# Final RMSNorm of a bidirectional encoder: products with the scale vector on VectorE between the small steps of 1/rms

## The chip, the cores and the metric

The kernel runs on one core of a Trainium2 chip. The metric is the device time of one execution in microseconds (us); lower is better. Engines are named as in the profile: PE is TensorE (matrix products), PEld its weight loads, DVE is VectorE, ACT is ScalarE, POOL is GpSimd, SP is SyncE, which here only starts transfers.

## The reference

Two encoder layers over 512 tokens of width 1024, in float32. Each layer adds three blocks to the residual stream x, and a norm ends it:

```python
for l in range(DEPTH):          # DEPTH = 2
    x = x + 0.5 * swiglu(rms_norm(x, ffn1_norm[l]), ffn1_w_in[l], ffn1_w_out[l])
    x = x + mixer(rms_norm(x, mix_norm[l]), ...)     # attention and a 2-D DFT, gated
    x = x + 0.5 * swiglu(rms_norm(x, ffn2_norm[l]), ffn2_w_in[l], ffn2_w_out[l])
return rms_norm(x, final_norm)

def rms_norm(x, g):
    y = x * rsqrt(mean(x * x, axis=-1) + 1e-6)
    return y * g
```

Only the end of it matters here: the last product of the last SwiGLU, which completes x, and the last `rms_norm`, whose result is the output. For each token that norm needs the sum of squares of all 1024 values before any of them can be scaled.

## The kernel before

**Layout.** x lies in SBUF as 128 partitions by 4 token blocks (`tb` 0 to 3) by 1024 columns; a column half `i` (0 or 1) has 512 columns. A token pair `j` is the blocks 2j and 2j+1. Every product is made from float32 values split into a high and a low part (`split`: ACT writes the high part at L288, DVE writes the difference at L289) and takes three matmuls (L282 high by high, L283 high activation by low weight, L284 low activation by high weight). A weight is loaded as a 128x1024 tile `raw` of 512 KB and split into `whi` and `wlo`, three buffers each, shortly ahead of its use (`Stream`, `Item.prep`).

**The last product.** The output product of the SwiGLU is made by Strassen's seven products, m = 1, 2, 5, 6, 7, 3, 4, each in three chunks c of the inner dimension (tiles c1h/c1l and so on are the split activations; `at` and `comb` at L593 make the sums that they are split from). `update` at L599 adds a finished product from PSUM to x, one token block at a time. Product 3 completes token blocks 2 and 3; product 4, the last, completes blocks 0 and 1 in column half 0, which is all that is then missing. Its third chunk runs `by_block`: the twelve matmuls of block 0 first, then the twelve of block 1.

**The final norm.** `nxt` is a `Norm` with `idx` 6. `squares` (L325, ACT, into `ssq`) sums squares of one block and one half. For blocks 2 and 3 `rstd` makes 1/rms (tile `r`) with an integer guess and three Newton steps on DVE, all on 128x2 tiles. For blocks 0 and 1 the generator `inverse` does the same on 128x1 tiles, in steps that other work can be put between. `gained` (L771) writes o = x * gf, where gf is the scale vector, fetched at L764; `scaled` (L776, ACT) multiplies o by 1/rms and starts the store of 256 KB from ACT's queue (L777); `whole` (L781, DVE) does both products in one instruction for the very last piece and stores from SP's queue (L782).

**Who sets the order.** Most instructions are put in order by a scheduler; inside `tc.manual_schedule` DVE and ACT keep the order in which the code is written, and `tc.high_priority` pulls a piece forward. In the kernel before, six `gained` products stand on POOL: four for blocks 2 and 3 and the second halves of blocks 0 and 1, written after chunk 0 of product 4; after them come the chain of `rstd` for blocks 2 and 3 and their four scalings. The manual block at the end holds blocks 0 and 1.

Of the kernel before, what the change touches and what calls it, by code (L numbers as in the profile page):

```python
# [9 lines left out]
F32 = mybir.dt.float32  # L10
# [3 lines left out]
AF = mybir.ActivationFunctionType  # L14
ALU = mybir.AluOpType
AX = mybir.AxisListType

P = 128
D = 1024
T = 512  # L20
# [7 lines left out]
EPS = 1e-6  # L28
# [64 lines left out]
def encoder_kernel(  # L93
    ctx: ExitStack, tc: tile.TileContext, xin, xtr, wst, gains, gfin, gbias, rpb, dft, chan, mask, ident_in, rot, out
):
    nc = tc.nc
# [16 lines left out]
    def slot(dt=F32, s="k", shape=(4, 256)):  # L113
        return kp.tile([P, *shape], dt, tag="k", name=nm(s), bufs=23)
# [39 lines left out]
    class Item:  # L154
# [9 lines left out]
        def prep(self):  # L164
            n = self.raw.n
            hi = wp.tile([P, 1024], F32R, tag="whi", name=nm("whi"), bufs=3)[:, 0:n]
            lo = wp.tile([P, 1024], F32R, tag="wlo", name=nm("wlo"), bufs=3)[:, 0:n]
            t = self.raw.t
            if self.add:
                V.tensor_tensor(t, t, self.add.t, ALU.add)  # L170
            if self.neg:
                S.activation(hi, t, AF.Copy, scale=-1.0)  # L172
                V.scalar_tensor_tensor(lo, t, -1.0, hi.bitcast(F32), ALU.mult, ALU.subtract)  # L173
            else:
                for c in range(0, n, n // self.parts):
                    cs = slice(c, c + n // self.parts)
                    split(hi[:, cs], lo[:, cs], t[:, cs])
            if self.then:
                G.dma_start(out=t, in_=wst[GRAN_AT[self.then]][:, 0:n], accum_op=ALU.add)
            self.out = (hi, lo)  # L180
# [65 lines left out]
    class Stream:  # L246
# [25 lines left out]
        def next(self):  # L272
            self.prep(self.pos + 1 + AHEAD)
            it = self.items[self.pos]
            self.pos += 1
            return it.out

    ws = Stream()
# [7 lines left out]
    def split(hi, lo, src, scale=None):  # L286
        if scale is None:
            S.activation(hi, src, AF.Copy)  # L288
            V.tensor_tensor(lo, src, hi.bitcast(F32), ALU.subtract)  # L289
        else:  # L290
            S.activation(hi, src, AF.Copy, scale=scale)
            V.scalar_tensor_tensor(lo, src, scale, hi.bitcast(F32), ALU.mult, ALU.subtract)


    def small(s, n=8):
        return sp.tile([P, 8], F32, tag=s, name=nm(s), bufs=2)[:, 0:n]

    def rsqrt(ms, n):
        r, t = small("r", n), small("rt", n)
        V.tensor_single_scalar(t.bitcast(I32), ms.bitcast(I32), 1, ALU.logical_shift_right)  # L300
        V.tensor_scalar(r.bitcast(I32), t.bitcast(I32), -1.0, float(0x5F3759DF), ALU.mult, ALU.add)
        for _ in range(3):
            V.tensor_tensor(t, r, r, ALU.mult)
            V.scalar_tensor_tensor(t, t, -0.5, ms, ALU.mult, ALU.mult)
            V.scalar_tensor_tensor(r, t, 1.5, r, ALU.add, ALU.mult)
        return r

    class Norm:

# [79 lines left out]
                V.tensor_scalar(r, t, 1.5, r, ALU.add, ALU.mult)  # L389
                yield  # L390

        def rstd(self, js=(0, 1)):

            n = 2 * len(js)
            a = 2 * js[0]
            ms = small("ms", n)
            with nullcontext() if self.idx == 6 else tc.high_priority():
                V.tensor_tensor(ms, self.ssq[:, a : a + n], self.ssq[:, 4 + a : 4 + a + n], ALU.add)
                V.tensor_scalar(ms, ms, 1.0 / D, EPS, ALU.mult, ALU.add)
                self.r = rsqrt(ms, n)  # L400
            if self.idx == 6:
                return self.r
            if self.mix:
                pc = bank()
                PE.matmul(pc[:, 0:2], mirror, self.r[:, 3:1:-1], start=True, stop=True)
                self.rflip = small("rflip", 2)
                V.tensor_copy(self.rflip, pc[:, 0:2])
                return
            self.rh, self.r2 = small("rh", 4), small("r2", 4)
            V.tensor_single_scalar(self.rh, self.r, 0.5, ALU.mult)  # L410
            V.tensor_tensor(self.r2, self.r, self.r, ALU.mult)
# [61 lines left out]
    def stage_ffn(norm, nxt, late):  # L473
# [122 lines left out]
        def update(ps, i, j, sign, bs=(0, 1)):  # L596
            for b in bs:
                v = x[:, 2 * j + b, i * T : (i + 1) * T]
                V.scalar_tensor_tensor(v, ps[b], 0.25 * sign, v, ALU.mult, ALU.add)  # L599
# [74 lines left out]
        for i, (m, c, _) in enumerate(steps):  # L674
            make(i)
            if i:
                make(i + 1)
            key = {6: 1, 4: 7}.get(m, m)
            if key not in ps:
                ps[key] = pair(f"o{key}")  # L680
            if m == 4 and c == 0 and nxt.mix:
                make(i + 2)
                ws.finish_stage()
                swap_pools(1)
            product(
                ps[key], made.pop(i), list(range(len(CHUNK[0][c]))), c == 0 and m in (1, 2, 3, 5, 7), c == 2,
                m in (4, 6), by_block=late and i == len(steps) - 1,
            )
            if i == 0:
                settle_at()  # L690
            if m == 4 and c == 0 and not late:
                with tc.manual_schedule(engines={mybir.EngineType.DVE, mybir.EngineType.Activation}):
                    make(i + 2)
                    nxt.quad(1, 1)
                    nxt.quad(0, 1)
            make(i + 2)
            if i == 6 and not late:
                nxt.quad(0, 0)
            if m == 4 and c == 1:
                update(ps[1], 1, 0, 1)  # L700
            if m == 4 and c == 0 and late:
                gains_of()
                for tb, i in ((2, 1), (3, 1), (2, 0), (3, 0), (0, 0), (1, 0)):
                    gained(G, tb, i)
                nxt.rstd((1,))
                for b in range(2):
                    nxt.inv[2 + b] = nxt.r[:, b : b + 1]
                    for i in (1, 0):
                        scaled(nxt, 2 + b, i)
            if c < 2:  # L710
                continue
            if m == 1:
                update(ps[1], 0, 0, -1)
            elif m == 2:
                update(ps[2], 0, 0, 1)
                nxt.squares(0, 0)
            elif m == 5:
                update(ps[5], 0, 1, 1)
                update(ps[5], 1, 1, -1)
            elif m == 6:  # L720
                update(ps[1], 1, 1, 1)
            elif m == 7:
                update(ps[7], 1, 1, 1)
                nxt.squares(1, 1)
                update(ps[1], 0, 1, -1)
            elif m == 3:
                update(ps[3], 0, 1, 1)
                nxt.squares(0, 1)
                if late:
                    make(i + 3)  # L730
            elif late:
                with tc.manual_schedule(engines={mybir.EngineType.DVE, mybir.EngineType.Activation}):
                    chain = [nxt.inverse(b) for b in range(2)]
                    for z in chain:
                        next(z)
                    update(ps[7], 1, 0, 1, (0,))
                    nxt.squares(1, 0, (0,))
                    gained(V, 0, 1)
                    next(chain[0])
                    update(ps[7], 1, 0, 1, (1,))  # L740
                    nxt.squares(1, 0, (1,))
                    for _ in chain[0]:
                        pass
                    scaled(nxt, 0, 0)
                    scaled(nxt, 0, 1)
                    for _ in chain[1]:
                        pass
                    scaled(nxt, 1, 0)
                    whole(nxt, 1, 1)
            else:  # L750
                update(ps[7], 1, 0, 1)
                nxt.squares(1, 0)
                nxt.later((1, 0))
# [1 line left out]
    gf = [None]  # L755
    ob = {}

    def half(tb, i):
        c = slice(i * T, (i + 1) * T)
        return ob[tb][:, c], x[:, tb, c], gf[0][:, c], out[:, tb, c]  # L760

    def gains_of():
        gf[0] = slot(F32, "gf", (D,))
        nc.sync.dma_start(out=gf[0], in_=bass.AP(tensor=gfin.tensor, offset=gfin.offset, ap=[[0, P], [1, D]]))  # L764

    def gained(engine, tb, i):

        if tb not in ob:
            ob[tb] = slot(F32, "o", (D,))
        o_, v, g, _ = half(tb, i)  # L770
        engine.tensor_tensor(o_, v, g, ALU.mult)  # L771

    def scaled(norm, tb, i):

        o_, _, _, to = half(tb, i)
        S.activation(o_, o_, AF.Copy, scale=norm.inv[tb])  # L776
        S.dma_start(out=to, in_=o_)  # L777

    def whole(norm, tb, i):
        o_, v, g, to = half(tb, i)  # L780
# [690 lines left out]
```

## Time and profile before

| | us |
|---|---|
| three timed runs | 1942.85, 1946.33, 1946.69 |
| median | 1946.33 |
| the profiled execution | 1946.85 |
| its span, first to last instruction | 1944.4 |
| outside the span | 2.45 |
| PE busy in the span | 1912.6 (98%) |
| DVE busy | 1624.1 (84%) |
| ACT busy | 1127.3 (58%) |
| POOL busy | 213.1 (11%) |

A busy PE row counts matmuls that overlap in the pipeline, so 98% is not the share of its peak. The times of rows below are us from the span's start. In a row of the timeline the first number is the start, the second the duration, then engine, line, operation, the tile written and those read, their shape, how many instructions were merged, and in brackets how long the engine had sat idle before it and what ended that. In a row of the waits view the numbers are the waited time in total, how often, and the longest. A row of the stretches view gives a stretch, its length, the busy time of each engine with its instructions, the granted clock of PE as a share of the full one, the share of time in which the 16 transfer engines moved data, and GB/s.

### The profile page before, as it was taken

The numbers are of one execution on the slowest core, as the hardware profiler recorded it, in microseconds if no ns is written. First come the engines' busy times: TensorE is split into PE (matmuls) and PEld (weight loads), VectorE is DVE, ScalarE is ACT, GpSimd is POOL, SyncE is SP. The second block draws the span as 40 slices with busy tenths as digits, with TensorE's granted clock in tenths as the row PEclk, the third lists the DMA queues.
The fourth block names the chain that finished last, engine by engine and source line by source line (L and its number), as shares of the span: only waits on it lengthen the run. The fifth ranks groups of instructions, "written<-read, shape, count | busy, mean of one in ns | idle before, by whom it ended". The sixth has DMA issues, their size and how long they took to land.

```text
span 1944.4 us, 24590 instructions
## 1 busy us (share of the span) xinstructions
PE 1912.6 (98%) x8997; PEld 1583.5 (81%) x8997; DVE 1624.1 (84%) x1945; ACT 1127.3 (58%) x1605; POOL 213.1 (11%) x252
## 2 busy tenths in 40 slices
PE   9999999999999999999999999999999999999996
PEld 7788888888778888888888888888887888888885
DVE  8878899698788877889977878996878887877998
ACT  6655666455556655566655556663555566555654
POOL 0001010300111010001000000102101110100012
PEclk9999999999999999999999999999999999999998
DMA  8777498321997567749857665965039975766692
GB/s 284 199 201 194 148 255 306 105 60 56 261 231 190 139 187 204 181 153 263 240 142 207 177 169 176 289 219 147 28 116 243 235 198 132 196 181 162 186 286 97
DMA packets 105448, 361.82 MB, mean 186 GB/s; under 512 B 12016, under 2 KB 14192, under 8 KB 105328
## 3 DMA queue, kind: packets, MB, share of 16 engines
q1 hardware_dynamic: 76848, 264.01, 39.7%
q0 software_dynamic: 27328, 94.39, 26.3%
q10 hardware_dynamic: 1152, 1.86, 0.3%
q8 instruction: 70, 1.15, 0.2%
q14 instruction: 50, 0.41, 0.1%
HBM read 354.97 MB, written 2.10 MB: 184 GB/s over the span
## 4 chain that ended last, share of the span: by engine, by line
PE 78%; DVE 13%; DMA 3%; issue 3%; ACT 3%; ACTq 0%; SPq 0%; POOL 0%; DVEq 0%; POOLq 0%
PE A L282 8%; PE A L284 8%; PE A L283 8%; PE o L283 5%; PE o L284 5%; PE o L282 5%; PE B L283 4%; PE B L284 4%; PE B L282 4%; PE ps L282 4%; PE ps L283 4%; PE ps L284 4%; DVE wlo L289 4%; DMA raw<-in_wst_dram 3%; PE C L283 2%
## 5 line engine op out<-in xcount | busy, mean ns | idle before, releaser
L289 DVE TENSOR_TENSOR wlo<-raw,whi 128x1024 fp32r<-128x1024 f32 (+1 forms) x522 | 628.1, 1209 | 252.9 <-ACT whi L288 251.9
L288 ACT ACTIVATE whi<-raw 128x1024 fp32r<-128x1024 f32 (+1 forms) x522 | 540.1, 1037 | 496.6 <-PE A L284 126.3
L152 POOL DMA_DIRECT2D raw<-in_wst_dram x152 | 131.2, 878 | 1338.4 <-DMA raw<-in_wst_dram 814.4
L170 DVE TENSOR_TENSOR raw<-raw,raw 128x1024 f32<-128x1024 f32 (+1 forms) x128 | 150.9, 1189 | 2.4
L283 PE MATMUL A<-wlo,xh 128*128 128x512 f32 x384 | 150.0, 391 | 2.8 <-DVE wlo L173 2.2
L284 PE MATMUL A<-whi,xl 128*128 128x512 f32 x384 | 149.6, 389 | 0.0
L282 PE MATMUL A<-whi,xh 128*128 128x512 f32 x384 | 149.4, 390 | 0.0
L172 ACT ACTIVATE whi<-raw 128x1024 fp32r<-128x1024 f32 x76 | 78.9, 1038 | 68.3 <-PE B L284 33.2
L173 DVE SCALAR_TENSOR_TENSOR wlo<-raw,whi 128x1024 fp32r<-128x1024 f32 x76 | 89.8, 1193 | 13.4 <-ACT whi L172 13.4
L283 PEld LDWEIGHTS A<-wlo,xh 128*128 128x128 f32 x384 | 72.1, 188 | 19.8 <-DVE wlo L173 4.0
L282 PEld LDWEIGHTS A<-whi,xh 128*128 128x128 f32 x384 | 71.9, 188 | 15.7 <-ACT whi L172 0.8
L284 PEld LDWEIGHTS A<-whi,xl 128*128 128x128 f32 x384 | 72.1, 188 | 14.9
L466 ACT ACTIVATE sn<-A 128x512 f32<-128x512 f32 x96 | 56.8, 598 | 41.8 <-PE A L284 41.7
L282 PE MATMUL A<-whi,t3h 128*128 128x512 f32 x192 | 75.1, 391 | 2.4 <-ACT sn L466 2.4
L282 PE MATMUL B<-whi,t1h 128*128 128x512 f32 x192 | 76.1, 398 | 0.4 <-ACT whi L288 0.4
L283 PE MATMUL A<-wlo,t2h 128*128 128x512 f32 x192 | 74.8, 390 | 0.5 <-DVE wlo L289 0.5
L283 PE MATMUL C<-wlo,xh 128*128 128x512 f32 x192 | 74.8, 390 | 0.5 <-DVE wlo L289 0.5
L283 PE MATMUL B<-wlo,t1h 128*128 128x512 f32 x192 | 75.0, 391 | 0.2
L282 PE MATMUL C<-whi,xh 128*128 128x512 f32 x192 | 74.8, 391 | 0.2 <-ACT whi L288 0.2
L282 PE MATMUL A<-whi,t2h 128*128 128x512 f32 x192 | 74.9, 392 | 0.0
L283 PE MATMUL A<-wlo,t3h 128*128 128x512 f32 x192 | 74.9, 390 | 0.0
L284 PE MATMUL B<-whi,t1l 128*128 128x512 f32 x192 | 74.9, 390 | 0.0
(352 smaller groups left out, 4944.1 us busy)
## 6 DMA issues: line engine op xcount, KB each, us to landing
raw<-in_wst_dram SPq DMA_DIRECT2D x463, 512.0 KB
raw<-in_wst_dram POOLq DMA_DIRECT2D x168, 512.0 KB, 7.8
raw<-in_wst_dram SPq DMA_DIRECT2D x30, 256.0 KB
vs<-v SPq DMA_DIRECT2D x12, 256.0 KB
bw<-in_rpb_dram SPq DMA_DIRECT2D x32, 68.0 KB
x<-in_xin_dram SPq DMA_DIRECT2D x4, 512.0 KB
raw<-in_wst_dram POOLq DMA_DIRECT2D x8, 256.0 KB, 8.4
dft<-in_dft_dram POOLq DMA_DIRECT2D x8, 256.0 KB, 5.4
```

The costliest lines, as they stand in the source:

```text
L152: G.dma_start(out=self.t, in_=wst[GRAN_AT[self.plus]][:, 0 : self.n], accum_op=ALU.add)
L170: V.tensor_tensor(t, t, self.add.t, ALU.add)
L172: S.activation(hi, t, AF.Copy, scale=-1.0)
L173: V.scalar_tensor_tensor(lo, t, -1.0, hi.bitcast(F32), ALU.mult, ALU.subtract)
L282: PE.matmul(ps, lh, rh, start=start, stop=False, skip_group_check=again)
L283: PE.matmul(ps, lh, rl, start=False, stop=False, skip_group_check=again)
L284: PE.matmul(ps, ll, rh, start=False, stop=stop, skip_group_check=again)
L288: S.activation(hi, src, AF.Copy)
L289: V.tensor_tensor(lo, src, hi.bitcast(F32), ALU.subtract)
L466: S.activation(t[:, b, :], ps[b], AF.Copy)
```

## The change

All six POOL products go to DVE. The chain of 1/rms for blocks 2 and 3 becomes a generator (`roots`, with a yield after every step of `rsqrt`), and the block at the end, which is now told to stand behind the split of the last weight (`issue_after` the last `wlo`), weaves the products between its steps: four products for blocks 2 and 3 in the first half of that chain, and those of block 0 and the first half of block 1 between the Newton steps of block 0. On ACT the squares of block 0 and of block 1 now stand ahead of the scalings; blocks 2, 3 and 0 are scaled by one 128x1024 instruction each instead of two of 128x512, and stored as 512 KB from SP's queue instead of twice 256 KB from ACT's. Block 1 keeps a half on ACT (`scaled`, stored from ACT's queue) and a half on DVE (`whole`, stored from SP's). The fetch of gf stays behind the last weight load in SP's queue. PE's instructions are the same and in the same order.

```diff
-    def rsqrt(ms, n):
-        r, t = small("r", n), small("rt", n)
+    def rsqrt(ms, r, t):
         V.tensor_single_scalar(t.bitcast(I32), ms.bitcast(I32), 1, ALU.logical_shift_right)
+        yield
         V.tensor_scalar(r.bitcast(I32), t.bitcast(I32), -1.0, float(0x5F3759DF), ALU.mult, ALU.add)
+        yield
...
             if m == 4 and c == 0 and late:
-                gains_of()
-                for tb, i in ((2, 1), (3, 1), (2, 0), (3, 0), (0, 0), (1, 0)):
-                    gained(G, tb, i)
-                nxt.rstd((1,))
-                for b in range(2):
-                    nxt.inv[2 + b] = nxt.r[:, b : b + 1]
-                    for i in (1, 0):
-                        scaled(nxt, 2 + b, i)
+                gf[0] = slot(F32, "gf", (D,))
+                nc.sync.dma_start(out=gf[0], in_=bass.AP(tensor=gfin.tensor, offset=gfin.offset, ap=[[0, P], [1, D]]))
...
-                with tc.manual_schedule(engines={mybir.EngineType.DVE, mybir.EngineType.Activation}):
+                with (
+                    tc.issue_after(ws.items[-1].last.ins),
+                    tc.manual_schedule(engines={mybir.EngineType.DVE, mybir.EngineType.Activation}),
+                ):
+                    ready = nxt.roots(2, 2)
+                    for tb, i in ((2, 0), (2, 1), (3, 0), (3, 1)):
+                        next(ready)
+                        gained(tb, i)
+                        next(ready)
                     chain = [nxt.inverse(b) for b in range(2)]
                     for z in chain:
                         next(z)
+                    for _ in ready:
+                        pass
+                    for b in range(2):
+                        nxt.inv[2 + b] = nxt.r[:, b : b + 1]
                     update(ps[7], 1, 0, 1, (0,))
                     nxt.squares(1, 0, (0,))
-                    gained(V, 0, 1)
+                    scaled(nxt, 2)
+                    gained(0, 0)
+                    next(chain[0])
+                    gained(0, 1)
+                    next(chain[0])
+                    gained(1, 0)
                     next(chain[0])
                     update(ps[7], 1, 0, 1, (1,))
                     nxt.squares(1, 0, (1,))
                     for _ in chain[0]:
                         pass
-                    scaled(nxt, 0, 0)
-                    scaled(nxt, 0, 1)
+                    scaled(nxt, 3)
+                    scaled(nxt, 0)
                     for _ in chain[1]:
                         pass
                     scaled(nxt, 1, 0)
...
-    def scaled(norm, tb, i):
+    def scaled(norm, tb, i=None):
         o_, _, _, to = half(tb, i)
         S.activation(o_, o_, AF.Copy, scale=norm.inv[tb])
-        S.dma_start(out=to, in_=o_)
+        (S if i is not None else nc.sync).dma_start(out=to, in_=o_)
```

More of the change, by code (lines that the diff above doesn't have):

```diff
@@ L176, in prep @@
                     cs = slice(c, c + n // self.parts)
-                    split(hi[:, cs], lo[:, cs], t[:, cs])
+                    self.last = split(hi[:, cs], lo[:, cs], t[:, cs])
             if self.then:
@@ L288, in split @@
             S.activation(hi, src, AF.Copy)
[L289 to L292, printed above, removed]
+            return V.tensor_tensor(lo, src, hi.bitcast(F32), ALU.subtract)
+        S.activation(hi, src, AF.Copy, scale=scale)
+        return V.scalar_tensor_tensor(lo, src, scale, hi.bitcast(F32), ALU.mult, ALU.subtract)
     def small(s, n=8):
         return sp.tile([P, 8], F32, tag=s, name=nm(s), bufs=2)[:, 0:n]
-    def rsqrt(ms, n):
-        r, t = small("r", n), small("rt", n)
+    def rsqrt(ms, r, t):
         V.tensor_single_scalar(t.bitcast(I32), ms.bitcast(I32), 1, ALU.logical_shift_right)
+        yield
         V.tensor_scalar(r.bitcast(I32), t.bitcast(I32), -1.0, float(0x5F3759DF), ALU.mult, ALU.add)
+        yield
         for _ in range(3):
             V.tensor_tensor(t, r, r, ALU.mult)
+            yield
             V.scalar_tensor_tensor(t, t, -0.5, ms, ALU.mult, ALU.mult)
+            yield
             V.scalar_tensor_tensor(r, t, 1.5, r, ALU.add, ALU.mult)
-        return r
+            yield
     class Norm:
@@ L390, in inverse, with roots, rstd @@
                 yield
[L392 to L402, printed above, removed]
+        def roots(self, a, n):
+            ms, self.r, t = small("ms", n), small("r", n), small("rt", n)
+            V.tensor_tensor(ms, self.ssq[:, a : a + n], self.ssq[:, 4 + a : 4 + a + n], ALU.add)
+            yield
+            V.tensor_scalar(ms, ms, 1.0 / D, EPS, ALU.mult, ALU.add)
+            yield
+            yield from rsqrt(ms, self.r, t)
+        def rstd(self):
+            with tc.high_priority():
+                for _ in self.roots(0, 4):
+                    pass
             if self.mix:
@@ L735, in stage_ffn @@
                         next(z)
+                    for _ in ready:
+                        pass
+                    for b in range(2):
+                        nxt.inv[2 + b] = nxt.r[:, b : b + 1]
                     update(ps[7], 1, 0, 1, (0,))
                     nxt.squares(1, 0, (0,))
-                    gained(V, 0, 1)
+                    scaled(nxt, 2)
[4 more added lines that the diff above has]
+                    gained(1, 0)
                     next(chain[0])
@@ L756, in encoder_kernel, with half, gained @@
     ob = {}
-    def half(tb, i):
-        c = slice(i * T, (i + 1) * T)
+    def half(tb, i=None):
+        c = slice(0, D) if i is None else slice(i * T, (i + 1) * T)
         return ob[tb][:, c], x[:, tb, c], gf[0][:, c], out[:, tb, c]
[L762 to L766, printed above, removed]
+    def gained(tb, i):
         if tb not in ob:
@@ L770, in gained @@
         o_, v, g, _ = half(tb, i)
-        engine.tensor_tensor(o_, v, g, ALU.mult)
-    def scaled(norm, tb, i):
+        V.tensor_tensor(o_, v, g, ALU.mult)
+    def scaled(norm, tb, i=None):
         o_, _, _, to = half(tb, i)
         S.activation(o_, o_, AF.Copy, scale=norm.inv[tb])
-        S.dma_start(out=to, in_=o_)
+        (S if i is not None else nc.sync).dma_start(out=to, in_=o_)
     def whole(norm, tb, i):
```

## The prediction

> **What bounds the kernel now.** I read the page first: PE is busy for 98% of the span, and the chain that ended last is 78% PE. Only the last 40 us differ between the two kernels, so I turned to the waits of that stretch. PE waits there once, and it is the longest wait of PE in the whole span:
>
> ```profile
> PE o L283 <- DVE wlo L289: 5.3, 1, 5.3
> ACT whi L288 <- DVE ms L399: 6.1, 1, 6.1
> ACT o L776 <- DVE r L305: 4.3, 1, 4.3
> ```
>
> Next, DVE's timeline there, and POOL's:
>
> ```profile
> 1908.63 3.22 DVE L289 TENSOR_TENSOR wlo<-raw,whi 128x1024 fp32r<-128x1024 f32 x2
> 1911.77 1.22 DVE L593 TENSOR_TENSOR at<-at,at 128x1024 f32<-128x1024 f32 x1
> 1912.90 1.28 DVE L599 SCALAR_TENSOR_TENSOR x<-o,x 128x512 f32<-128x512 f32 x2
> 1914.10 1.94 DVE L593 TENSOR_TENSOR at<-at,at 128x1024 f32<-128x1024 f32 x1
> 1915.96 2.28 DVE L289 TENSOR_TENSOR c4l<-at,c4h 128x1024 fp32r<-128x1024 f32 x1
> 1918.16 2.28 DVE L289 TENSOR_TENSOR wlo<-raw,whi 128x1024 fp32r<-128x1024 f32 x1
> 1920.37 2.29 DVE L289 TENSOR_TENSOR c4l<-at,c4h 128x1024 fp32r<-128x1024 f32 x1
> 1922.58 1.21 DVE L289 TENSOR_TENSOR wlo<-raw,whi 128x1024 fp32r<-128x1024 f32 x1
> ```
>
> ```profile
> 1907.76 3.54 POOL L771 TENSOR_TENSOR o<-x,gf 128x512 f32<-128x512 f32 x2 [19.54 <-DMA gf<-in_gfin_dram]
> 1913.66 7.92 POOL L771 TENSOR_TENSOR o<-x,gf 128x512 f32<-128x512 f32 x4 [2.37 <-DVE x L599]
> ```
>
> The reader is to see one pair: a two-input DVE instruction of 128x1024 takes 1.22 us in POOL's pause (1911.30 to 1913.66) and 2.28 us while a POOL product runs. DVE is delayed by POOL, PE waits for the `wlo` that ends at 1920.44, and while it waits its clock is halved:
>
> ```profile
> 1915.25:1917.90 2.65, 0.00 (x0) 0.00 (x0) 2.65 (x2) 1.88 (x3) 2.65 (x2) 1.00 0.00 0
> 1917.90:1920.50 2.60, 0.00 (x0) 0.00 (x1) 2.60 (x3) 1.12 (x2) 2.60 (x2) 0.50 0.00 0
> 1920.50:1924.70 4.20, 4.20 (x10) 3.33 (x11) 4.20 (x4) 0.00 (x0) 1.08 (x1) 0.50 0.00 0
> ```
>
> Last, ACT's end, which sets the last stores:
>
> ```profile
> 1933.99 0.63 ACT L325 ACTIVATE junk<-x 128x512 bf16<-128x512 f32 x1 [0.41 <-ACT o L776]
> 1936.53 0.63 ACT L325 ACTIVATE junk<-x 128x512 bf16<-128x512 f32 x1 [1.81 <-DVE x L599]
> 1940.66 0.34 ACTq L777 DMA_DIRECT2D out_dram<-o  x1
> ```
>
> The update of block 0 starts at 1930.51, but its squares only at 1933.99, behind four scalings with their store starts.
>
> **Part 1, POOL's products go.** From 1908.63 I lay DVE's unchanged order out again, at 1.13 us from start to start for 128x1024 and 0.60 for 128x512 (durations 1.22 and 0.68 less the overlap of 0.08). The split pair at 1908.63 takes 1.73, `at` starts at 1910.36, the two updates of x at 1911.49, the second `at` at 1912.69, c4l at 1913.82, `wlo` at 1914.95; it ends at 1916.16 where it ended at 1920.44. ACT keeps up: its `whi` for this one starts at 1910.80, held by PE, in both. PE's wait of 5.25 us becomes 0.97 (1915.25 to 1916.22). PE waited 0.99, 0.91 and 0.90 us at 53, 1466 and 506 us, and the granted clock there is 1.00, so I expect no halved clock. Ten matmuls then need 2.3 us (0.227 from start to start) and not 4.3, and the last `whi`, which waits for their buffer, starts at 1918.75, was 1925.10.
>
> DVE goes on: c4l 1916.08, two `wlo` to 1919.47, an update of x, the last `wlo` 1920.07 to 1921.20, an update, free at 1921.80. The last `whi` is ready at 1919.83, 0.24 before DVE asks for it. PE ends block 0's matmuls at 1924.1 (was 1930.48).
>
> **Part 2, what DVE takes on.** In the changed order 21 instructions stand between 1921.80 and the update of block 0: four products and 17 small steps. A product costs 0.60 (row 1931.24: 0.69 long). A small step that needs the one before it costs 0.20 (L303 to L305 at 1929.25, 1929.44, 1929.64), another 0.07 (1928.67, 1928.73). Nine dependent, seven others and the last 0.07: 2.40 + 1.80 + 0.56 = 4.76. The bounds are 17 at 0.07 and 17 at 0.20, so 3.6 to 5.8. The update starts at 1926.56, 2.5 us after PE is ready: DVE, not PE, is late next. Against 1930.51 the gain here is 3.95.
>
> One rule speaks against taking work back. The Trainium skill, "Perfetto Trace Analysis", section "Optimizing Scalar/DVE Operations", says that a saturated DVE may be relieved to ScalarE or even GpSimd, but warns that the two share a read port. Here the pair 1.22 and 2.28 sides with the warning.
>
> **Part 3, ACT and the chains.** Block 0: squares start 0.72 after the update (1935.81 to 1936.53), `ms` 0.75 later (1933.99 to 1934.74), at 1928.03. Its chain with two products between the Newton steps: 1.07 + 0.60 + 0.43 + 0.60 + 0.43 = 3.13, so block 1's update starts at 1931.16 (was 1935.81), PE long done. Product (0,0) hides behind the squares. Squares of block 1: 1931.88 to 1932.61, `ms` 1932.63 (was 1937.40).
>
> Queued behind those squares on ACT, though ready since 1926.5, is the scaling of block 3. No row shows 128x1024 with a scale per partition; 0.72 for half plus 0.42 (1.04 less 0.62, the splits L288) gives 1.14, between 1.04 and 1.44. Block 3 is scaled to 1933.76, block 0 to 1934.9. Added wait: block 1's tile `r` takes over the buffer that holds blocks 2 and 3's 1/rms, so its first write (ready 1933.07) waits for block 3's scaling, to 1933.80; the rest of its chain is queued behind. From there 1.86 (1937.83 to 1939.69): `whole` and ACT's half start at 1935.66, their stores at 1936.46.
>
> **Part 4, the stores.** Before, 1 MB is left for the end, now 1.57 MB: 512 KB of block 3 started at 1933.82, 512 KB of block 0 at 1934.95, two halves of block 1 at 1936.46. SP has nothing else queued; its three starts cost ACT nothing, where ACT lost 0.42 per store. Data follows 0.85 after the start. This stretch gives the rate:
>
> ```profile
> 1941.35:1942.75 1.40, 0.00 (x0) 0.00 (x0) 0.00 (x0) 0.00 (x0) 0.00 (x0) 0.50 0.96 363
> ```
>
> At full share that is 378 GB/s. Data from 1934.67, never out of work: 1.57 MB takes 4.16, to 1938.83, which also covers the added wait by 0.13. From the last data (1942.84) to the end were 1.56: the span ends at 1940.39. Bounds for the stores: no limit by rate, 1939.56; 290 GB/s, as the stretch 1932 to 1934 moved with its pauses, 1941.65.
>
> **Sum.** 1944.40 to 1940.39 is a gain of 4.0 us: 3.95 up to block 0's update, 0.8 more to block 1's `ms`, 0.7 given back by the stores. From the profiled execution's own 1946.85 that is 1942.85. It stands 0.5 above the median, so 1942.3 against 1946.33.
>
> A measurement of this kernel can tell about 0.2%, 3.9 us, from no change. My gain sits on that line.
>
> **Rivals.**
>
> *A, the gain is there but under the line (chance 0.27).* Stores at 290 GB/s: gain 2.75. All small steps at 0.20: gain 3.0. Both and 1.44 per scaling: 1.4, so 1944.9. For it: three sizes that no row shows. Against: each is taken from the nearest row.
>
> *B, the halved clock isn't in every run of before (0.18).* The three runs differ by 3.8 us, which speaks for something that comes and goes. Without the drop the last `whi` is 2 us earlier, but then DVE's `ms` at 1924.92 is ahead of the last `wlo`: that starts at 1924.99 for 1926.19, 1.2 us gained. If the median run had no drop, the gain is 2.8: 1943.5. The Trainium skill, "TensorE: Matmul & The Clock Gate", section "What's actually happening", says the clock falls after one idle window of about 3.4 us that runs freely. By that an idle time of 5.25 us holds a whole window only in some runs, and 0.97 in none; this trace agrees with one drop, 2.65 us into the wait, and none at 0.99. Should the drop stay in the changed kernel, its last `wlo` comes 1.8 later: 1944.1.
>
> *C, slower: the 2.28 isn't POOL's doing (0.06).* If DVE's two-input instructions are slow at that place for another reason, part 1 gives nothing: DVE is free at 1927.93 as before, and the six products on its path cost 2.24 each. Then block 0's update starts at 1927.93 + 4.76 + 4 x 1.62 = 1939.2, and with two more slow products the end lies 11.8 later: 1958. It decides from 0.92 us per product. Against it: the 1.22 in POOL's pause, and DVE's own product at 1931.24 with 0.69.
>
> That the change doesn't take place is excluded by the order of the instructions: POOL has no product left, PE's order is the same.
>
> **Numbers.** Forecast, a gain from 3.9 up: 0.47, with the bounds 3.6 for part 2 and 1939.56 for the stores up to 5.9 us, 1940.4. A and B: 0.45 together, C and what I overlook: 0.08. Faster 0.47, within 0.45, slower 0.08. Range: 1940.4 less 1.2 for runs like the fast one shown, 1939.2, to A's 1944.9 plus 0.9, 1945.8; C stays out.
>
> **What would show it.** DVE rows of 1.21 from 1908 to 1922; PE's wait near 1 us at clock 1.00; DVE's update of block 0 near 1926.6, behind 21 instructions without a wait; block 3's scaling right behind block 1's squares; SP's stores near 1933.8 and 1935, data without a pause. It is wrong if the two-input rows stay above 2, if PE's clock drops, or if a store starts after 1937.

## The result, and the profile after

| | before | changed |
|---|---|---|
| median of 22 runs each, us | 1944.55 | 1941.66 |
| lowest to highest | 1942.49 to 1950.29 | 1939.12 to 1945.16 |
| the profiled execution | 1946.85 | 1942.89 |
| its span | 1944.4 | 1940.9 |

The ratio of the times is 0.9981, 95% interval 0.9975 to 0.9987. At 1944.55 that is 3.7 us gained, between 2.5 and 4.9; the two medians differ by 2.9. So the change is a gain beyond doubt, but on which side of 0.2% it lies these runs do not tell.

The two profiled executions do not reach the end at the same pace: a row that the change does not touch, DVE's three merged updates of x ahead of the last weights, starts at 1906.83 before and at 1907.58 changed. I take that row as **the mark** and count from it: 37.57 us to the end of the span before, 33.27 changed, so 4.3 us gained behind the mark (the expectations below write 33.32, reckoned from the span as rounded in the table). A time of the prediction is to be compared with a row of the changed kernel less 0.75.

DVE's timeline of the changed kernel (line numbers have moved: the updates of x are L605, the products L784, the last piece L794):

```profile
1907.58 1.88 DVE L605 SCALAR_TENSOR_TENSOR x<-o,x 128x512 f32<-128x512 f32 x3
1909.38 1.82 DVE L289 TENSOR_TENSOR wlo<-raw,whi 128x1024 fp32r<-128x1024 f32 x2
1913.45 1.22 DVE L599 TENSOR_TENSOR at<-at,at 128x1024 f32<-128x1024 f32 x1
1914.58 1.22 DVE L289 TENSOR_TENSOR c4l<-at,c4h 128x1024 fp32r<-128x1024 f32 x1
1915.72 1.22 DVE L289 TENSOR_TENSOR wlo<-raw,whi 128x1024 fp32r<-128x1024 f32 x1
...
1922.59 0.15 DVE L398 TENSOR_TENSOR ms<-ssq 128x2 f32<-128x2 f32 x1
...
1927.31 0.68 DVE L605 SCALAR_TENSOR_TENSOR x<-o,x 128x512 f32<-128x512 f32 x1
...
1931.97 0.68 DVE L605 SCALAR_TENSOR_TENSOR x<-o,x 128x512 f32<-128x512 f32 x1
1933.50 0.21 DVE L386 TENSOR_SCALAR ms<-ssq,e 128x1 f32<-128x1 f32 x1 [0.85 <-ACT junk L328]
...
1934.54 0.15 DVE L389 TENSOR_SCALAR r<-rt 128x1 int32<-128x1 int32 x1 [0.51 <-ACT o L789]
...
1936.40 0.75 DVE L794 SCALAR_TENSOR_TENSOR o<-x,r,gf 128x512 f32<-128x512 f32 x1
```

Every 128x1024 row is back at 1.22. From 1922.59 to 1927.31 stand the 21 instructions that DVE took on; the two updates behind them belong to blocks 0 and 1. The two bracketed rows are the only idle times shown here: one for the squares, one for the buffer of `r`. Two rows of the waits view of this stretch:

```profile
PE o L283 <- DVE wlo L289: 1.0, 1, 1.0
...
DVE r L389 <- ACT o L789: 0.5, 1, 0.5
```

PE's wait of 5.3 us has become 1.0. The stretches view (length, busy time of PE, PEld, DVE, ACT and POOL, then PE's clock, the share of time with data, GB/s):

```profile
1915.00:1920.00 5.00, 4.01 (x18) 3.02 (x17) 5.00 (x5) 3.02 (x4) 0.00 (x0) 1.00 0.00 0
1920.00:1925.00 5.00, 5.00 (x24) 4.14 (x23) 4.93 (x12) 0.70 (x1) 0.00 (x0) 1.00 0.00 0
```

```profile
1935.37:1939.54 4.17, 0.00 (x0) 0.00 (x0) 1.65 (x5) 0.90 (x2) 0.00 (x0) 0.50 0.96 377
```

The clock stays at 1.00 through the stretch where it was halved, POOL is at 0, and the last stores run without a pause at 377 GB/s. ACT's timeline of the end shows squares in front and scalings behind:

```profile
1928.09 0.63 ACT L328 ACTIVATE junk<-x 128x512 bf16<-128x512 f32 x1 [7.39 <-DVE x L605]
1928.72 1.13 ACT L789 ACTIVATE o<-o,r 128x1024 f32<-128x1024 f32 x1
1932.75 0.63 ACT L328 ACTIVATE junk<-x 128x512 bf16<-128x512 f32 x1 [2.90 <-DVE x L605]
1933.38 2.17 ACT L789 ACTIVATE o<-o,r 128x1024 f32<-128x1024 f32 x2
```

Block 0's squares start 0.78 us after its update starts; it was 3.48 (1930.51 to 1933.99).

### The profile page after: what moved, and what is told of

Its sections match the earlier page's. It is cut to its first block, busy times and chain, and to the rows that moved or that the text cites. A ratio compares the mean times of both kernels' runs of the same rounds, so it can differ in the third digit from the quotient of the medians.

```text
span 1940.9 us, 24584 instructions
## 1 busy us (share of the span) xinstructions
PE 1911.7 (98%) x8997; PEld 1582.2 (82%) x8997; DVE 1621.7 (84%) x1951; ACT 1126.2 (58%) x1602; POOL 201.8 (10%) x246
## 4 chain that ended last, share of the span: by engine, by line
PE 77%; DVE 14%; issue 3%; DMA 3%; ACT 2%; POOL 0%; ACTq 0%; DVEq 0%; POOLq 0%
PE A L282 8%; PE A L284 8%; PE A L283 8%; PE B L283 4%; PE B L284 4%; PE o L283 4%; PE B L282 4%; PE o L284 4%; PE o L282 4%; DVE wlo L289 4%; PE ps L282 4%; PE ps L283 4%; PE ps L284 4%; DMA raw<-in_wst_dram 3%; PE C L283 2%
## 5 line engine op out<-in xcount | busy, mean ns | idle before, releaser
L283 PE MATMUL B<-wlo,xh 128*128 128x512 f32 x192 | 74.8, 390 | 0.1
```

The lines of the kernel that those rows point to most:

```text
L283: PE.matmul(ps, lh, rl, start=False, stop=False, skip_group_check=again)
```

## The experiments

All of them are counted from the same mark, each in one profiled execution. The last two columns are the ratio to the kernel before in timed runs on the same chip, and the number of runs.

| kernel | update of block 0 | block 1's squares | end of span | ratio (95%) | runs |
|---|---|---|---|---|---|
| before | 23.68 | 29.70 | 37.57 | 1 | 22 |
| before, second profile | 23.48 | 29.50 | 37.37 | | 1 |
| before, third profile | 23.83 | 29.21 | 37.07 | | 1 |
| changed | 19.73 | 25.17 | 33.27 | 0.9981 (0.9975 to 0.9987) | 22 |
| changed, second profile | 19.72 | 25.16 | 33.28 | 0.9982 (0.9973 to 0.9990) | 11 |
| products on DVE, ACT as before | 19.72 | 28.99 | 36.86 | 1.0003 (0.9994 to 1.0011) | 11 |
| ACT changed, products on POOL | 24.01 | 28.99 | 37.11 | 0.9992 (0.9982 to 1.0001) | 11 |
| block 3 scaled early | 19.73 | 25.17 | 32.74 | 0.9980 (0.9971 to 0.9989) | 11 |
| updates first | 17.46 | 21.11 | 31.60 | 0.9972 (0.9961 to 0.9984) | 6 |
| updates first, again | 17.45 | 21.09 | 31.59 | 0.9973 (0.9962 to 0.9984) | 7 |

My theory: POOL's products slow DVE, DVE holds PE, and beside that ACT's scalings hold block 0's squares; the change removes both. Rivals: the gain belongs to one of the two alone; or POOL is not what slows DVE (C); or it comes from the clock only and so comes and goes (B).

**Products on DVE, ACT as before.** Half of the change is undone: blocks 2 and 3 are again scaled in four halves, with ACT starting their stores, ahead of block 0's squares, and block 0 in two halves. The order on ACT, the whole-block scalings and the stores from SP's queue thus go together; no run here tries them apart.

```diff
                         nxt.inv[2 + b] = nxt.r[:, b : b + 1]
+                    for b in range(2):
+                        for i in (1, 0):
+                            scaled(nxt, 2 + b, i)
                     update(ps[7], 1, 0, 1, (0,))
                     nxt.squares(1, 0, (0,))
-                    scaled(nxt, 2)
...
-                    scaled(nxt, 3)
-                    scaled(nxt, 0)
+                    scaled(nxt, 0, 0)
+                    scaled(nxt, 0, 1)
```

> DVE's order and products as in the changed kernel, POOL without products; but ACT again scales blocks 2 and 3 in four halves ahead of block 0's squares and stores all halves but one from its own queue, as before. Measure: from the start of DVE's three merged updates of x ahead of the last splits (1906.83 before, 1907.58 changed) to the end of the span: 37.57 us before, 33.32 changed. My theory: DVE rows stay at 1.22, PE's wait at 1 us, the update of block 0 at 19.7 from the mark as in the changed kernel; then four scalings with a store start each (1.14 apiece, row 1937.57 to 1938.71) hold block 0's squares 3.9 us longer, so 36.6: nearly all of the gain goes. Rival, that taking POOL's products away is the gain and ACT's order a detail: 33.3 to 34.5. Rival C, two-input DVE instructions are slow at that place whatever POOL does: rows of 2.28.

Measured: 36.86 from the mark to the end, so 0.71 gained of 4.3; in timed runs no difference that the interval can tell. DVE's timeline and, behind it, ACT's:

```profile
1915.10 1.22 DVE L289 TENSOR_TENSOR wlo<-raw,whi 128x1024 fp32r<-128x1024 f32 x1
...
1926.69 0.68 DVE L605 SCALAR_TENSOR_TENSOR x<-o,x 128x512 f32<-128x512 f32 x1
...
1932.12 0.21 DVE L386 TENSOR_SCALAR ms<-ssq,e 128x1 f32<-128x1 f32 x1 [4.14 <-ACT junk L328]
```

```profile
1930.98 0.34 ACTq L792 DMA_DIRECT2D out_dram<-o  x1
1931.36 0.63 ACT L328 ACTIVATE junk<-x 128x512 bf16<-128x512 f32 x1 [0.41 <-ACT o L791]
```

The update of block 0 comes as early as in the changed kernel (19.72), and then DVE waits 4.14 us for squares that stand behind four scalings. In one point the kernel is not as before. There ACT's scalings ran in pairs with the store starts behind them:

```profile
1930.48 1.34 ACT L776 ACTIVATE o<-o,r 128x512 f32<-128x512 f32 x2 [4.33 <-DVE r L305]
1932.24 1.34 ACT L776 ACTIVATE o<-o,r 128x512 f32<-128x512 f32 x2 [0.42 <-ACT o L776]
```

Four took 3.51 us (1930.48 to 1933.99); here a store start stands behind each, and they take 4.55 (1926.81 to 1931.36). So 1.04 us of its loss is due to the order that I wrote, and not to the change.

**ACT changed, products on POOL.** The other half undone: six products on POOL again, ACT and SP as in the changed kernel. The Newton steps on DVE keep the order of the changed kernel too.

```diff
                 nc.sync.dma_start(out=gf[0], in_=...)
+                for tb, h in ((2, 1), (3, 1), (2, 0), (3, 0), (0, 0), (1, 0)):
+                    gained(tb, h, G)
...
                     ready = nxt.roots(2, 2)
-                    for tb, i in ((2, 0), (2, 1), (3, 0), (3, 1)):
-                        next(ready)
-                        gained(tb, i)
-                        next(ready)
...
-                    gained(0, 0)
...
-                    gained(1, 0)
...
-    def gained(tb, i):
+    def gained(tb, i, engine=V):
...
-        V.tensor_tensor(o_, v, g, ALU.mult)
+        engine.tensor_tensor(o_, v, g, ALU.mult)
```

> The six products back on POOL where they stood, ACT's order, the whole-block scalings and SP's stores as in the changed kernel. Same measure (37.57 before, 33.32 changed). My theory: DVE rows of 2.28 again, PE's wait 5.25 with the halved clock if the free-running window falls so, the update of block 0 24.0 from the mark as before; then block 0's squares at once, but the stores of 1.57 MB start at 30.6 and take 4.2, so 37.2: hardly any gain. Rival, that ACT's order and the stores are the gain: 34 to 35. The clock row also shows whether the drop is in every execution.

Measured: 37.11, which is 0.46 less than in the first profile of the kernel before and no less than in its third (37.07); so no gain is shown, and the timed runs show none that the interval can tell. DVE's timeline, POOL's, the waits and the stretches of this kernel:

```profile
1906.19 1.87 DVE L605 SCALAR_TENSOR_TENSOR x<-o,x 128x512 f32<-128x512 f32 x3
1907.98 2.90 DVE L289 TENSOR_TENSOR wlo<-raw,whi 128x1024 fp32r<-128x1024 f32 x2
1910.81 1.21 DVE L599 TENSOR_TENSOR at<-at,at 128x1024 f32<-128x1024 f32 x1
...
1915.00 2.29 DVE L289 TENSOR_TENSOR c4l<-at,c4h 128x1024 fp32r<-128x1024 f32 x1
1917.21 2.28 DVE L289 TENSOR_TENSOR wlo<-raw,whi 128x1024 fp32r<-128x1024 f32 x1
```

```profile
1906.66 2.55 POOL L780 TENSOR_TENSOR o<-x,gf 128x512 f32<-128x512 f32 x2 [18.91 <-DMA gf<-in_gfin_dram]
1912.70 7.92 POOL L780 TENSOR_TENSOR o<-x,gf 128x512 f32<-128x512 f32 x4 [3.50 <-DVE x L605]
```

```profile
PE o L283 <- DVE wlo L289: 4.6, 1, 4.6
```

```profile
1917.00:1919.50 2.50, 0.00 (x0) 0.00 (x0) 2.50 (x3) 1.06 (x2) 2.50 (x2) 0.77 0.00 0
1919.50:1923.70 4.20, 4.15 (x10) 3.28 (x11) 4.20 (x3) 0.00 (x0) 1.13 (x1) 0.50 0.00 0
```

With the products back on POOL, the rows of 2.28, PE's wait and the halved clock are back, in another kernel and on another run. Rival C is out from both sides: these rows take 1.22 in every kernel without POOL's products, and 2.28 beside them in every kernel with them. The squares of block 0 now follow its update at once, but that update comes at 24.01.

**The two halves and the whole.** The path up to block 1's squares, cut into its stretches (each is the difference of two starts). Three starts of the kernel before, the two updates and the last product:

```profile
1930.51 0.69 DVE L599 SCALAR_TENSOR_TENSOR x<-o,x 128x512 f32<-128x512 f32 x1
1935.81 0.68 DVE L599 SCALAR_TENSOR_TENSOR x<-o,x 128x512 f32<-128x512 f32 x1
1939.69 0.75 DVE L781 SCALAR_TENSOR_TENSOR o<-x,r,gf 128x512 f32<-128x512 f32 x1
```

| us | before | changed | products on DVE only | ACT only |
|---|---|---|---|---|
| mark to update of block 0 | 23.68 | 19.73 | 19.72 | 24.01 |
| on to its squares (ACT) | 3.48 | 0.78 | 4.67 | 0.79 |
| on to `ms` | 0.75 | 0.75 | 0.76 | 0.75 |
| on to update of block 1 (DVE) | 1.07 | 3.13 | 3.13 | 2.66 |
| on to its squares | 0.72 | 0.78 | 0.71 | 0.78 |
| sum | 29.70 | 25.17 | 28.99 | 28.99 |

The change gains twice, 3.95 on DVE and PE and 2.70 on ACT, and pays 2.06 in the fourth row: two products and two more Newton steps now stand ahead of block 1's update. Either half alone, as I cut them, has one gain and pays most of the price: 3.96 less 2.06, less 1.19 on ACT (1.04 of it my order), leaves 0.71; 2.69 less 1.59, less 0.33 and 0.06 in the first and last rows, leaves 0.71, of which 0.46 reach the end. That is why neither half is worth much and both are. The column before is its first profile. In the other two the first two rows are 23.48 and 3.48, 23.83 and 2.85; their sum, 27.16 in the table, is 26.96 and 26.68 there, so terms of a few tenths are not settled by one profile each.

**Block 3 scaled early.** Takes away the wait for the buffer of `r`, by scaling block 3 right behind block 2.

```diff
                     scaled(nxt, 2)
+                    scaled(nxt, 3)
...
-                    scaled(nxt, 3)
                     scaled(nxt, 0)
```

> The changed kernel with block 3 scaled right behind block 2, in the 2.9 us in which ACT waits for block 1's update. Same measure (33.32 changed). My theory: block 3's store leaves 3.5 us earlier, the wait of DVE's chain for the r buffer (0.51) goes, block 0 and block 1 follow 0.6 earlier and the last data no longer queue: 32.7. Rival, that the end is set by the rate of the stores and not by the chain: 1 MB instead of 1.57 MB behind the same start, so more, 31.8. Rival, that neither binds: 33.3.

Measured: 32.74, 0.53 earlier than the changed kernel. ACT's timeline:

```profile
1927.36 2.17 ACT L789 ACTIVATE o<-o,r 128x1024 f32<-128x1024 f32 x2
...
1931.40 0.63 ACT L328 ACTIVATE junk<-x 128x512 bf16<-128x512 f32 x1 [1.86 <-DVE x L605]
```

Both scalings fit into ACT's idle time ahead of block 1's squares, and these still wait for DVE. The last product starts 0.60 us earlier behind the mark (1934.45 less 1906.23, against 1936.40 less 1907.58), so the wait for the buffer of `r` lay on the path. This kernel also takes 512 KB out of the last run of stores, but that was not what held the end: from the last product to the last data are 3.14 us in the changed kernel and 3.12 here. In timed runs 0.5 us cannot be told from the changed kernel.

**Updates first.** If DVE is what is late after the change, and not PE, then the products should stand behind the two updates. DVE's order here: the chain of 1/rms for blocks 2 and 3 with steps of `inverse` in its gaps, block 0's update, the two products of block 2, `ms` and the first Newton step, block 1's update, and the other products between later steps. `inverse` gets one more yield, behind its first step.

```diff
...
                     ready = nxt.roots(2, 2)
-                    for tb, i in ((2, 0), (2, 1), (3, 0), (3, 1)):
-                        next(ready)
-                        gained(tb, i)
-                        next(ready)
                     chain = [nxt.inverse(b) for b in range(2)]
-                    for z in chain:
+                    for z in (*chain, *chain):
+                        next(ready)
                         next(z)
...
                     update(ps[7], 1, 0, 1, (0,))
                     nxt.squares(1, 0, (0,))
+                    gained(2, 0)
+                    gained(2, 1)
                     scaled(nxt, 2)
-                    gained(0, 0)
-                    next(chain[0])
-                    gained(0, 1)
-                    next(chain[0])
-                    gained(1, 0)
                     next(chain[0])
                     update(ps[7], 1, 0, 1, (1,))
                     nxt.squares(1, 0, (1,))
-                    for _ in chain[0]:
-                        pass
+                    gained(3, 0)
+                    next(chain[0])
+                    gained(3, 1)
                     scaled(nxt, 3)
...
```

> The same instructions as the changed kernel in another order on DVE: behind the last split first the chain of blocks 2 and 3 with the small steps of the other chains in its gaps, then the update of block 0, and that of block 1 after the first Newton step of block 0; the products go between the later steps, ACT scales each block when its product is there. Same measure (33.32 changed, 37.57 before). My theory (DVE, not PE, is late at the update of block 0 in the changed kernel by 2.5 us): the update of block 0 starts 2.2 us earlier, at 17.5 from the mark, that of block 1 near 20.4 instead of 24.4, and the span ends at 31.3. Rival, that PE sets the updates: they wait for PE, and the end stays at 33 or later.

Measured: 31.60. DVE's timeline of this kernel:

```profile
1908.10 1.88 DVE L606 SCALAR_TENSOR_TENSOR x<-o,x 128x512 f32<-128x512 f32 x3
...
1925.56 0.69 DVE L606 SCALAR_TENSOR_TENSOR x<-o,x 128x512 f32<-128x512 f32 x1
...
1928.43 0.68 DVE L606 SCALAR_TENSOR_TENSOR x<-o,x 128x512 f32<-128x512 f32 x1
...
1935.01 0.75 DVE L795 SCALAR_TENSOR_TENSOR o<-x,r,gf 128x512 f32<-128x512 f32 x1
```

The updates of blocks 0 and 1 come at 17.46 and 20.33 (changed: 19.73 and 24.39): what stood ahead of them was DVE's own work. The last matmul of block 0 shows how late DVE had been, first in the changed kernel, then in this one:

```profile
1924.60 0.39 PE L284 MATMUL o<-whi,c4l 128*128 128x512 f32 x1
```

```profile
1925.13 0.39 PE L284 MATMUL o<-whi,c4l 128*128 128x512 f32 x1
```

PE ends block 0 at 17.41 and 17.42 from the mark. In the changed kernel DVE's update comes 2.32 us behind that, here 0.04. Of the 4.06 won at block 1's update 1.67 arrive at the end, chiefly because five products are still to be made behind it. A second measurement was made to see whether the timed runs bear that out:

> The order with both updates first again, beside the changed kernel: 31.6 from the mark to the end, 1.7 us less than the changed kernel; ratio to before near 0.997 (6 of 1945 us).

> The changed kernel again beside the next one on the same chip: 33.3 from the mark to the end, ratio to before near 0.998 (4.2 of 1945 us).

Measured: 31.59 beside 33.28, on the same chip; ratios 0.9973 and 0.9982 to the same kernel before. By the profile this version beats both kernels, by 1.7 and 6.0 us behind the mark. The timed intervals overlap, 0.9962 to 0.9984 against 0.9973 to 0.9990, so that it is faster than the changed kernel is shown by the traces (two profiles of each) and not by the timed runs.

**Is the halved clock always there?** Two more profiles of the kernel before, with no edit, for rival B.

> The kernel before, unchanged: one more look at PE's long wait. Rival B says that the halved clock isn't in every execution (a window of about 3.4 us that runs freely fits into 5.25 us of waiting only in some): then some look shows clock 1.00 through the wait and an end 1.2 us nearer to the mark of DVE's three merged updates (36.4 instead of 37.57). Against B: the drop is in every look, at different distances from the start of the wait.

> The same once more: 37.6 from the mark to the end with the halved clock, 36.4 without.

Measured: both have the wait, and both the drop. PE's timeline and the stretches of the first, then the stretches of the second:

```profile
1918.87 0.79 PE L283 MATMUL o<-wlo,c4h 128*128 128x512 f32 x1 [5.04 <-DVE wlo L289]
```

```profile
1913.82:1916.32 2.50, 0.00 (x1) 0.00 (x0) 2.50 (x2) 1.88 (x2) 2.50 (x2) 1.00 0.00 0
1916.32:1918.87 2.55, 0.00 (x1) 0.00 (x1) 2.55 (x3) 1.07 (x2) 2.55 (x2) 0.50 0.00 0
1918.87:1923.15 4.28, 4.28 (x10) 3.42 (x11) 4.28 (x4) 0.00 (x0) 1.07 (x1) 0.50 0.00 0
```

```profile
1914.63:1918.21 3.58, 0.00 (x0) 0.00 (x0) 3.58 (x3) 2.95 (x3) 3.58 (x3) 1.00 0.00 0
1918.21:1919.22 1.01, 0.00 (x0) 0.00 (x0) 1.01 (x2) 0.00 (x0) 1.01 (x1) 0.50 0.00 0
```

The clock falls 2.50 and 3.58 us into the wait, 2.65 in the first profile and 3.35 in the kernel with the products back on POOL: four profiled executions of four. The ends behind the mark are 37.37 and 37.07 beside 37.57, so among these three executions of the kernel before, all with the drop, half a microsecond varies there, not 3.8.

The timed runs say more, since each has its mean granted clock on record. In the three profiles of before it is 0.9967, 0.9967 and 0.9962; the 6.83 us of the drop at half clock make 0.0018 of that, so a run without the drop would show 0.998 (an estimate from these profiles). Of the 45 timed runs of before on the two chips of the experiments, 39 show 0.996 or 0.997 and 6 show 0.998; of the 11 with the products back on POOL, 3 show 0.998, the two fastest among them. So by this reckoning the drop is missing in some runs, about one in seven of before. Of the 33 runs of the changed kernel 26 show 0.998 and none 0.996. Wait and drop come together in all four profiles, so what each costs by itself no run here separates.

## Why the prediction was right

**Part 1** held. Predicted was a wait of 0.97 us at a full clock; it is 0.99 in the first profile, at 1.00. (In the second profile of the changed kernel it is 0.34, without a change of the end.)

**Part 2** held. The 21 instructions take 4.72 us (1922.59 to 1927.31), predicted 4.76. Block 0's update at 1927.31 less 0.75 is 1926.56, the very number. PE ends block 0 at 17.41 from the mark, where the prediction had 17.3 (1924.1 less 1906.83). So DVE is late by 2.32 us, predicted 2.5, and the kernel with the updates first confirms it: its update starts at 17.46.

**Part 3** held. Block 1's update stands at 1931.22 in the time of before (predicted 1931.16), its `ms` at 1932.75 (1932.63). The scaling of 128x1024 takes 1.13, predicted 1.14. The wait for the buffer of `r`, counted as the prediction did from when its first write was ready (0.43 behind `ms`), is 0.61 and not 0.73 (the profile's row has 0.51, as it counts from the end of DVE's instruction ahead); `ms` came 0.12 later. The last product starts at 1935.65 (1935.66).

**Part 4** held in its rate. From the first data of the last stores to the last are 4.17 us, predicted 4.16, at 377 GB/s where I had taken 378. One term was mis-sized: from the last data to the end of the span are 1.31, not 1.56. That is nearly all of why the gain behind the mark is 4.3 and not 4.0. It goes with the kernel: 1.56 to 1.57 in the three profiles of before, 1.30 to 1.31 in the two of the changed one; why is not shown. And the "0.7 given back by the stores" is put down to the wrong thing. From the start of the last product to the last data are 3.15 us before and 3.14 in the changed kernel, so the larger stores cost nothing there; what is given back between block 1's `ms` and the last product is 0.61, the wait for the buffer of `r`. The prediction has that wait among its rows (0.73) and holds that the stores cover it by 0.13; the two were close, and the kernel with block 3 scaled early shows which one held the end.

**The sum and the median.** 4.3 was measured in the first pair of profiles. The three profiles of the kernel before end at 37.57, 37.37 and 37.07, on average 37.34, and the two at the changed one at 33.27 and 33.28; that leaves 4.06. The timed gain of 3.7 (2.5 to 4.9) agrees. That the predicted median of 1942.3 is so close to 1941.66 is partly luck: the three runs that it was reckoned from had a median of 1946.33, and the 22 runs of the same kernel have 1944.55. So the medians differ by 2.9 where 4.0 was forecast, inside the timed interval.

**Where the reasoning was thin.** The sum writes 3.95 for the update of block 0, as the gain of taking POOL's work away, and adds the rest. Read so, the DVE part alone would bring nearly all of it; it brought 0.71, or some 1.75 (an estimate: 0.71 and the 1.04 of my order) with ACT exactly as before; against the mean of the three profiles of before both are 0.23 less. The "0.8 more to block 1's `ms`" is right as a net (0.70 by the rows) but hides two larger terms of opposite sign, 2.70 gained on ACT and 2.06 paid on DVE. A sum that had shown them would have pointed at the order of the products, which the kernel with the updates first changes.

**The rivals.** A's terms are all refuted by rows: stores at 377 GB/s and not 290, 4.72 for the small steps, 1.13 per scaling. Its outcome, a gain that the timing cannot tell from 0.2%, is nevertheless what the timed ratio shows, since the forecast itself lay on that line. B's premise is borne out in part: the drop was in each of four profiled executions, but the mean clocks of the timed runs speak for some runs without it, 6 of 45. So most runs have it, and B's reason, a median run without it, does not hold, though the medians differ by 2.9 and B's gain was 2.8. Nor is the drop what spreads the runs: the kernel with the products on DVE and ACT as before, which has no drop in its profile, still spreads over 8.2 us (1942.97 to 1951.17). What makes the runs of one kernel differ by 6 us and more stays open; a part of it lies ahead of the stretch studied, as the mark itself stands between 1905.4 and 1908.6 in these profiles. C falls by two experiments, above.

## What to carry to other kernels

Before crediting an edit with the time by which one instruction comes earlier, look what its consumer is doing at that time, and what the edit puts between the two: here neither half of a two-part change was worth more than 0.7 us and both together some 4, since each paid most of the price of the new order. When two engines slow each other, compare the same instruction inside and outside of the other's pause; one pair of rows (1.22 and 2.28) carried the whole first part of this forecast. And after a wait is gone, order the new bound's work by who waits for it: putting the updates ahead of the products was worth 1.7 us more in the profile.

## What the runs showed of the hardware

**DVE and POOL.** In the kernel with the products back on POOL, the split pair of DVE at 1907.98 takes 2.90 us instead of 1.82, while the updates of x at 1906.19 take 1.87 for three, as without POOL, though a POOL product starts at 1906.66 beside them. The updates have one operand in PSUM, the splits have both in SBUF; they are also different operations, and no run here tries the one operation with the operands of the other. The Trainium skill, "SBUF — State Buffer", section "Who interferes with whom", says that a DVE instruction with two SBUF inputs contends with a GpSimd instruction that reads SBUF, and that one with at most one does not, outside the modes that use both of DVE's ports. The rows agree, and they add a price: in turns, a DVE instruction of 1.22 takes 2.28, and four POOL products take 7.92, so 1.98 each, where two ran in 2.55. That each is held for a whole instruction of the other fits these rows but was not tried by itself.

**The clock.** Each of the four drops lasts 6.83 us (1916.32 to 1923.15 and 1918.21 to 1925.04 in the two further profiles of before), whatever its start. They begin 2.50 to 3.58 us into a wait of PE of 4.6 to 5.3 us, and there is none at waits of 0.99 us. The Trainium skill, "TensorE: Matmul & The Clock Gate", section "What's actually happening", puts the drop after an idle window of some 3.4 us that runs freely. A length of 6.83 is twice 3.4, which fits; but two of the four drops begin well before PE had been idle for 3.4 us (2.50 and 2.65, a third at 3.35), so if that is the window, it was not idle throughout. In this the prediction read its trace too kindly: a drop 2.65 us into a wait does not agree with a whole idle window of 3.4. Its reading that only some runs have the drop is borne out, but not in its share: by the page's window, 5.25 us would hold a whole one in about half of the runs (an estimate: 5.25 less 3.4, over 3.4), and by the mean clocks 39 of 45 had the drop.
